# A two-layer hybrid diffusion trunk on one core: a fourth load buffer, and the last half-step's front one token tile at a time

## The chip, the core and the metric

The kernel runs on one core of a Trainium2 chip. Its engines are TensorE (PE, with PEld for loading the stationary operand), VectorE (DVE), ScalarE (ACT), GpSimd (POOL) and SyncE (SP), which here issues nearly all DMAs. The metric is the device time of one execution in microseconds (us), the median of several runs. TensorE's clock has two levels, 1.2 and 2.4 GHz; the profile gives the granted clock of a stretch as a share of the higher.

## The reference

The inputs are 256 latent tokens `x`, 256 context tokens `ctx`, a conditioning vector `c`, and the weights of two layers; width 1024, hidden width 2816, everything in float32. Each layer is a SwiGLU half-step, token mixing, and another SwiGLU half-step. Every sub-layer reads a normalised, shifted and scaled input and is added back through a gate:

```python
def sandwich_in(x, mods, idx, g_pre):
    shift, scale = mods[3 * idx], mods[3 * idx + 1]
    return rms_norm(x, g_pre) * (1 + scale) + shift
def sandwich_out(x, y, mods, idx, g_post, res_w):
    gate = mods[3 * idx + 2]
    return x + res_w * gate * rms_norm(y, g_post)
def swiglu(h, w1, w2):
    a, b = jnp.split(h @ w1, 2, axis=-1)
    return (jax.nn.silu(a) * b) @ w2
```

The nine modulation vectors of a layer come from `c` through one more matrix (adaLN, 1024 x 9216). Token mixing projects to 16 slices of 128 channels, runs four heads of neighbourhood attention, four pooling groups and four heads of differential attention, each differential head with its own normalisation behind it, and projects the 1024 joined channels back with `w_out`. After the last layer only the 256 latent tokens are returned, so its last half-step has 256 tokens, in two tiles of 128.

## The kernel before

All products keep float32 accuracy by splitting each operand into a high and a low part of TensorE's float32 format; a product is then three matmuls, high x high, low x high and high x low. Weights arrive as units of 512 kB: SP issues a DMA into a raw buffer (L179, L204), ACT copies the high part into a slot (L186), DVE subtracts to get the low part (L191). There are three raw buffers, `raw0` to `raw2`, used in a ring: the load of unit k may go once unit k-3 has been split. adaLN weights use the same ring but are not split; DVE multiplies them by the conditioning and adds them up (L464, L466; eight operations per unit), and every four units TensorE sums over partitions (`red`), ACT copies the row (L474), and TensorE transposes it (L482, `fin`). Slots lie in three tiles `w` and in the large tile `R`, which at other times holds mixing data.

The order is made when the kernel is built. `schedule` merges a main list of steps with side lists by due times; `run` then writes the instructions, each step's loads and splits a little ahead of the step, the loads as far ahead as the ring lets them. A load that waits for its buffer holds SP's queue; a split that waits for its data holds ACT's.

A half-step has 22 hidden tiles of 128. For a hidden tile, `pair` takes two units of `w1` as the stationary operand (128 x 128 blocks) and lets the tokens move: with the last half-step's 256 tokens 2 x 8 x 3 = 48 matmuls of 128 x 256. `hidden` follows: silu on ACT (L590), the product with the second half on DVE (L591), the high part on ACT (L593) and the low part on DVE (L594). The first four pairs are the *front* and stand ahead of the others, because their units are loaded while the mixing still runs.

Before the last half-step stands the last out-projection, `wout_rows`: eight rows of `w_out` in the order of the heads that become ready, six matmuls of 128 x 512 for each row and token tile. The last head is the differential head 7; its subtraction L1009 ends the wait. Behind a tile's last row `tok_end` squares (L519), multiplies by the gate (L521), takes the root (DVE L506, POOL L507), adds to the stream `X` (L524), squares and roots again (L525) and writes the normalised rows `YB` (L526). Then `pre_pair`, once for each quarter of the channels and for both token tiles together, transposes `YB` (L536), applies shift and scale on ACT (L539), and splits into `HH` (L540) and `HL` (L541). The front's matmuls come next. The step `late` held some of its `w1` splits back to 4 us behind the out-projection in the planner's count.

## Time and profile before

| | us |
|---|---|
| median of 3 runs | 1832.28 (1830.18 to 1832.47) |
| profiled execution, its own time | 1824.12 |
| its span, first to last instruction | 1822.3 |
| TensorE busy in the span | 1750.3 (96%) |
| DVE / ACT / POOL busy | 1170.7 / 714.8 / 72.8 |
| mean granted clock | 0.987 |
| DMA moved | 260.19 MB, 143 GB/s over the span |

The profile is of one execution. Busy times are sums of instructions; a window's busy time compared with its length says how long the engine had nothing to do there. PE's matmuls overlap, so their single lengths do not add up, and the pace is read from how many start in a stretch. A wait of PE is put down to the instruction whose result it waited for last.

### The profile page before, as it was taken

To read this page: it belongs to the slowest core of one execution; us is meant where nothing else is said; L and a number is where in the kernel's file an instruction comes from. 1 tells how busy PE (TensorE), PEld (TensorE's weight loads), DVE (VectorE), ACT (ScalarE), POOL (GpSimd) and SP (SyncE) were. 2 spreads that over 40 slices of the span, in tenths; PEclk is the share of its full clock that TensorE was granted. 3 is DMA by queue.
4 is the path that set the end of the run, shared out by engine and by line. 5 is a ranking of instruction groups with operands and counts; after the bars stand their busy time and mean duration, and the time that the engine had idled before them with its cause. 6 is when DMAs were issued, how large, how long until landed. Compare 5 with 4: busy or idle time off the path is not lost.

```text
span 1822.3 us, 24374 instructions
## 1 busy us (share of the span) xinstructions
PE 1750.3 (96%) x9496; PEld 1452.9 (80%) x9496; DVE 1170.7 (64%) x1889; ACT 714.8 (39%) x1244; POOL 72.8 (4%) x128
## 2 busy tenths in 40 slices
PE   4999999999999999999999999999999999969998
PEld 3788777778977779878878798888887897859997
DVE  4756776667367875757758565666765737865553
ACT  3323222235267763323222442322223526654442
POOL 0000000001000400000000000000000100200000
PEclk8999999999999999999999999999999999979999
DMA  7836555554211152656545334645554431255662
GB/s 230 243 116 192 176 173 157 167 171 125 57 47 47 64 171 71 188 163 182 176 148 176 124 105 127 197 122 183 176 161 156 115 69 58 93 151 187 187 187 76
DMA packets 301187, 260.19 MB, mean 143 GB/s; under 512 B 18064, under 2 KB 246160, under 8 KB 301072
## 3 DMA queue, kind: packets, MB, share of 16 engines
q1 hardware_dynamic: 297216, 257.67, 46.5%
q8 instruction: 74, 1.21, 0.3%
q10 hardware_dynamic: 3856, 0.97, 0.2%
q14 instruction: 41, 0.34, 0.1%
HBM read 257.51 MB, written 1.10 MB: 142 GB/s over the span
## 4 chain that ended last, share of the span: by engine, by line
PE 65%; DMA 14%; DVE 12%; ACT 5%; issue 3%; POOL 1%; SPq 0%; ACTq 0%; DVEq 0%; POOLq 0%
PE bank L90 62%; DMA raw<-in_ffn_w_dram 10%; DVE sx L466 3%; DVE R L191 2%; ACT R L186 2%; DVE w L191 2%; DMA raw<-in_w_ada_dram 2%; ACT w L186 1%; DMA gtb<-in_w_ada_dram 1%; POOL sr L507 1%; PE bank L802 1%; PE bank L536 1%; DMA csrc<-in_c_dram 1%; DVE sx L464 0%; DVE X L524 0%
## 5 line engine op out<-in xcount | busy, mean ns | idle before, releaser
L90 PE MATMUL bank<-HH,R 128*128 128x512 f32 (+1 forms) x2028 | 531.7, 347 | 4.7 <-ACT R L186 2.5
L90 PE MATMUL bank<-HH,w 128*128 128x512 f32 (+1 forms) x1540 | 433.9, 359 | 0.4 <-DVE w L191 0.4
L90 PEld LDWEIGHTS bank<-HH,R 128*128 128x128 f32 x2028 | 356.3, 191 | 59.5 <-issue 7.2
L90 PE MATMUL bank<-R 128*128 128x512 f32 (+3 forms) x1632 | 364.1, 376 | 2.9 <-DVE YB L642 1.1
L90 PE MATMUL bank<-HL,R 128*128 128x512 f32 (+1 forms) x1014 | 349.5, 345 | 0.0
L90 PEld LDWEIGHTS bank<-R 128*128 128x128 f32 (+1 forms) x1632 | 278.5, 188 | 74.0 <-issue 9.7
L191 DVE TENSOR_TENSOR R<-raw,R 128x1024 fp32r<-128x1024 f32 (+1 forms) x177 | 214.7, 1216 | 173.5 <-ACT R L186 170.1
L466 DVE SCALAR_TENSOR_TENSOR sx<-raw,sc,sx 128x512 f32<-128x512 f32 x448 | 310.8, 745 | 21.8 <-DMA raw<-in_w_ada_dram 21.4
L186 ACT CAST R<-raw 128x1024 fp32r<-128x1024 f32 (+1 forms) x177 | 184.3, 1043 | 343.3 <-DMA raw<-in_ffn_w_dram 270.3
L90 PEld LDWEIGHTS bank<-HH,w 128*128 128x128 f32 x1540 | 274.1, 190 | 50.2 <-issue 12.0
L191 DVE TENSOR_TENSOR w<-raw,w 128x1024 fp32r<-128x1024 f32 (+1 forms) x153 | 187.5, 1226 | 161.8 <-ACT w L186 161.5
L90 PE MATMUL bank<-HL,w 128*128 128x512 f32 (+1 forms) x770 | 274.7, 357 | 0.0
L186 ACT CAST w<-raw 128x1024 fp32r<-128x1024 f32 (+1 forms) x153 | 159.9, 1046 | 279.8 <-DMA raw<-in_ffn_w_dram 199.6
L90 PE MATMUL bank<-w,R 128*128 128x512 f32 x960 | 236.0, 396 | 2.6 <-ACT R L1008 1.8
L90 PEld LDWEIGHTS bank<-w,R 128*128 128x128 f32 x960 | 178.1, 189 | 43.4 <-ACT R L1008 2.3
L90 PEld LDWEIGHTS bank<-HL,R 128*128 128x128 f32 x1014 | 193.3, 191 | 22.4 <-DVE HL L541 0.2
L90 PEld LDWEIGHTS bank<-HL,w 128*128 128x128 f32 x770 | 146.5, 190 | 20.6 <-issue 2.3
L591 DVE TENSOR_TENSOR sil<-sil,bank 128x512 f32<-128x512 f32 (+1 forms) x96 | 55.5, 578 | 77.9 <-PE bank L90 77.7
L593 ACT CAST R<-sil 128x512 fp32r<-128x512 f32 (+1 forms) x96 | 51.2, 533 | 135.0 <-DVE sil L591 135.0
L507 POOL TENSOR_TENSOR sr<-sr,eps 128x1 f32<-128x1 f32 x42 | 28.3, 674 | 1463.5 <-DVE sr L506 1444.5
L590 ACT ACTIVATE sil<-bank 128x512 f32<-128x512 f32 (+1 forms) x96 | 48.9, 510 | 90.7 <-PE bank L90 84.4
L360 DVE TENSOR_TENSOR R<-bank,R 128x512 fp32r<-128x512 f32 (+2 forms) x86 | 47.9, 561 | 33.8 <-ACT R L359 33.5
(145 smaller groups left out, 1211.8 us busy)
## 6 DMA issues: line engine op xcount, KB each, us to landing
raw<-in_ffn_w_dram SPq DMA_DIRECT2D x258, 512.0 KB
raw<-in_w_ada_dram SPq DMA_DIRECT2D x130, 512.0 KB
raw<-in_w_in_dram SPq DMA_DIRECT2D x40, 512.0 KB
raw<-in_w_out_dram SPq DMA_DIRECT2D x24, 512.0 KB
gtb<-in_w_ada_dram SPq DMA_DIRECT2D x10, 512.0 KB
gtb<-gate SPq DMA_DIRECT2D x10, 512.0 KB
raw<-in_ffn_w_dram SPq DMA_DIRECT2D x8, 384.0 KB
sx<-in_w_ada_dram SPq DMA_DIRECT2D x4, 512.0 KB
```

The source lines that it names most:

```text
L90: return nc.tensor.matmul(out=o, lhsT=l, rhs=r, start=start, stop=stop)
L186: ins = S.copy(out=self.hi, in_=self.raw)
L191: ins = self.lo_eng.tensor_tensor(out=self.lo, in0=self.raw, in1=self.hi.bitcast(F32), op=ALU.subtract)
L360: V.tensor_tensor(out=lo, in0=src, in1=hi.bitcast(F32), op=ALU.subtract)
L466: V.scalar_tensor_tensor(out=ACC[v], in0=u.raw[:, z, :], scalar=sv, in1=ACC[v], op0=ALU.mult, op1=ALU.add)
L507: G.tensor_tensor(out=a, in0=a, in1=mhalf, op=ALU.pow)
L536: nc.tensor.transpose(out=pt[:, z, t * P : (t + 1) * P], in_=y[:, t, k * P : (k + 1) * P], identity=ident)
L590: S.activation(out=sl[:, cs], in_=oa, func=AF.Silu)
L591: V.tensor_tensor(out=sl[:, cs], in0=sl[:, cs], in1=ob, op=ALU.mult)
L593: tab["hs"] = S.copy(out=uh[:, cs], in_=sl[:, cs])
L802: nc.tensor.transpose(out=b[:, n * P : (n + 1) * P], in_=e[:, n * P : (n + 1) * P], identity=ident)
```

## The change

1. A fourth raw buffer. Room for it comes from the scratch tile `junk`, which is halved, and from the place of one hidden tile in `R`.
2. adaLN: the transposes of a row (`fin`) are written two units later (`take`); the small loads of the gate's bias are written two units later too.
3. Layout of `R`: hidden units 0 to 7 lie in its first 8192 columns, the ninth at its end, and the load slots between, where they cover whole mixing tiles.
4. Last layer's `wout_rows`: its eight units have fixed slots, each free from a named mark in the mixing; rows 4 to 6 of token tile 1 become low-priority side steps, and its row 7 follows tile 0's.
5. Last half-step's front: token tile by token tile. `pre_tok` prepares half the channels of one tile. `front_tok` keeps `HH` and `HL` blocks of 128 tokens stationary and lets `w1` move, 512 columns at a time: 48 matmuls of 128 x 512 for each tile. The result has tokens on partitions, so `turned` applies silu and product, transposes four blocks and splits them from there into the hidden units. The `late` mark is gone.

```diff
-    raws = [tile(f"raw{i}", [1024]) for i in range(3)]
+    raws = [tile(f"raw{i}", [1024]) for i in range(4)]
-    JUNK = tile("junk", [D], mybir.dt.bfloat16)
+    JUNK = tile("junk", [T], mybir.dt.bfloat16)
-    U_HI = [R[:, i * 1024 : i * 1024 + T] for i in range(NU)]
+    U_AT = [i * 1024 for i in range(8)] + [19456]
+    U_HI = [R[:, i : i + T] for i in U_AT]
...
-                if j % 3 == 2:
-                    st.append(Step(lambda l=l, j=j, h=h: gate_rows(l, j, h)))
                 for q in range(4):
+                    if q == 2 and j % 3 == 2:
+                        st.append(Step(lambda l=l, j=j, h=h: gate_rows(l, j, h)))
...
+    def pre_tok(l, i, g, t, q):
+        ks, ts = slice(4 * q, 4 * q + 4), slice(GROUPS[g].start + t * P, GROUPS[g].start + (t + 1) * P)
+        pt, f = [z.rearrange("p (k t) -> p k t", k=4) for z in (XB(), S2())]
+        for z in range(4):
+            nc.tensor.transpose(out=pt[:, z], in_=y_of(g)[:, t, (4 * q + z) * P : (4 * q + z + 1) * P], identity=ident)
+        for z in range(4):
...
+            if z % 2:
+                V.tensor_scalar(out=f[:, z], in0=pt[:, z], scalar1=sc_, scalar2=sh, op0=ALU.mult, op1=ALU.add)
+            else:
+                S.activation(out=f[:, z], in_=pt[:, z], func=AF.Identity, scale=sc_, bias=sh)
+        V.tensor_copy(out=HH[:, ks, ts], in_=f)
+        V.tensor_tensor(out=HL[:, ks, ts], in0=f, in1=HH[:, ks, ts].bitcast(F32), op=ALU.subtract)
...
-        nf = 0 if done else FRONT
+        nf = 0 if done or not both else FRONT
...
+            fu = [[unit(w1[q * SEQ : (q + 1) * SEQ, h * DFF : h * DFF + T]) for h in range(2)] for q in range(4)]
+            for u in fu[0] + fu[1]:
+                u.after = f"nav{l}"
+            def turned(t, ts, oa, ob):
+                sl = SIL()
+                S.activation(out=sl, in_=oa, func=AF.Silu)
+                V.tensor_tensor(out=sl, in0=sl, in1=ob, op=ALU.mult)
+                pt = XB().rearrange("p (j t) -> p j t", j=4)
+                for j in range(4):
+                    nc.tensor.transpose(out=pt[:, j], in_=sl[:, j * P : (j + 1) * P], identity=ident)
+                u4 = R[:, 0:4096].rearrange("p (j x) -> p j x", j=4)
+                split_ps(u4[:, :, ts], u4[:, :, ts.start + T : ts.stop + T], pt)
...
+                            for oh, u in zip(o, fu[q]):
+                                mm(oh, HH[:, k, ts], u.hi[:, z], k == 0, False)
+                                mm(oh, HL[:, k, ts], u.hi[:, z], False, False)
+                                mm(oh, HH[:, k, ts], u.lo[:, z], False, k == KD - 1)
+                        if q == 3:
+                            turned(t, ts, *o)
...
+            if last:
+                n = 4
+                for i, sl in enumerate((0, 1, 2, 6, 4, 7, 5, 3)):
+                    us[i].slots = (sl,)
+                    if sl > 2:
+                        us[i].after = {6: f"nav{l}", 4: "dv0", 7: "qk0", 5: "dv1", 3: "pt"}[sl]
...
+                t0, t1 = [[row(i, t) for i in range(n, KD)] for t in range(2)]
+                for z in t1[:-1]:
+                    z.low = True
+                t1[-1].needs += t1[:-1]
+                return st + t0, t1, box
...
+            for s in f(*pieces.pop(0)):
+                if s.fin:
+                    late = [s, 2]
+                    continue
+                o.append(s)
+                if late:
+                    late[1] -= 1
+                    if not late[1]:
+                        o.append(late[0])
+                        late = []
...
-            late = Step(lambda: None, after=[(out_[LAT], 4.0)])
-            late.mark = "late"
-            schedule(main + wait_h(f[0][LAT], hl), [late] + hl + side)
+            for t, (end, bks) in enumerate(zip(out_["ends"], (lambda: banks[4:6], lambda: out_["box"]["b"][0]))):
+                main += [Step(lambda t=t, q=q: pre_tok(l, 2, LAT, t, q), dur=0.44, after=[(end, KN["wt"] + q)]) for q in range(2)]
```

Where the instructions stand, at three places. First TensorE at the first adaLN row behind the start, before the change (`rows` is the row that ACT copied, `cst` holds the identity, `bank` a PSUM bank):

```order
L90 MATMUL bank_104<-HL,R 128x512
L90 MATMUL bank_104<-HH,R 128x512
L482 MATMUL bank_106<-cst,rows 128x128 x2
L90 MATMUL bank_105<-HH,R 128x512
L90 MATMUL bank_105<-HL,R 128x512
L90 MATMUL bank_105<-HH,R 128x512 x2
```

and after it:

```order
L90 MATMUL bank_101<-HL,w_72 128x512
L90 MATMUL bank_101<-HH,w_72 128x512
L484 MATMUL bank_107<-cst,rows 128x128 x2
L90 MATMUL bank_101<-HH,w_72 128x512
L90 MATMUL bank_101<-HL,w_72 128x512
L90 MATMUL bank_101<-HH,w_72 128x512 x2
```

The transposes stood between two hidden tiles of one load and now stand 26 rows further on, among matmuls of a later unit; the other rows keep their order.

Next TensorE from the last rows of the last out-projection into the front, before:

```order
L90 MATMUL bank_103<-w_71,R 128x512 x2
L90 MATMUL bank_100<-w_71,R 128x512 x2
L90 MATMUL bank_101<-w_71,R 128x512 x2
L90 MATMUL bank_102<-w_71,R 128x512 x2
L536 MATMUL bank_106<-cst,YB 128x128
L536 MATMUL bank_107<-cst,YB 128x128
L536 MATMUL bank_106<-cst,YB 128x128 x3
L536 MATMUL bank_107<-cst,YB 128x128 x3
L536 MATMUL bank_106<-cst,YB 128x128 x4
L90 MATMUL bank_104<-HH,R 128x256
L90 MATMUL bank_104<-HL,R 128x256
L90 MATMUL bank_104<-HH,R 128x256 x2
```

and after, where the front's first tile begins, and where its second does:

```order
L90 MATMUL bank_101<-R 128x512 x2
L90 MATMUL bank_102<-R 128x512 x2
L90 MATMUL bank_103<-R 128x512 x2
L551 MATMUL bank_107<-cst,YB 128x128 x4
L551 MATMUL bank_108<-cst,YB 128x128 x4
L90 MATMUL bank_105<-w_72,HH 128x512
L90 MATMUL bank_105<-w_72,HL 128x512
L90 MATMUL bank_105<-w_72,HH 128x512
L90 MATMUL bank_106<-w_73,HH 128x512
```

```order
L90 MATMUL bank_106<-R,HH 128x512
L90 MATMUL bank_106<-R,HL 128x512
L90 MATMUL bank_106<-R,HH 128x512
L551 MATMUL bank_108<-cst,YB 128x128 x4
L698 MATMUL bank_107<-cst,sil_75 128x128 x4
L551 MATMUL bank_107<-cst,YB 128x128 x4
L90 MATMUL bank_104<-w_72,HH 128x512
L90 MATMUL bank_101<-w_73,HH 128x512
L90 MATMUL bank_104<-w_72,HL 128x512
L90 MATMUL bank_104<-w_72,HH 128x512
```

Before, transposes of both token tiles go ahead of a front whose weights in `R` are stationary. After, eight transposes of tile 0 go ahead of its 48 matmuls; behind them stand tile 1's first four, the four of `turned`, tile 1's other four, and then tile 1's 48.

Last DVE in the same place, from the end of tile 0 of the out-projection, before (L191 is a load's subtraction, L526 writes a tile's `YB`; tile 0 ends at the fifth row):

```order
L191 TENSOR_TENSOR w_71<-raw_69,w_71 128x1024
L524 SCALAR_TENSOR_TENSOR X<-s_77,sr_84,X 128x512 x2
L191 TENSOR_TENSOR w_73<-raw_68,w_73 128x1024
L506 SCALAR_TENSOR_TENSOR sr_84<-sr_84,eps 128x1
L526 TENSOR_SCALAR YB<-X,sr_84 128x1024
L191 TENSOR_TENSOR w_72<-raw_70,w_72 128x1024
L521 TENSOR_TENSOR s_77<-bank_101,gtb 128x512
L521 TENSOR_TENSOR s_77<-bank_102,gtb 128x512
L506 SCALAR_TENSOR_TENSOR sr_85<-sr_85,eps 128x1
L524 SCALAR_TENSOR_TENSOR X<-s_77,sr_85,X 128x512 x2
L506 SCALAR_TENSOR_TENSOR sr_85<-sr_85,eps 128x1
L526 TENSOR_SCALAR YB<-X,sr_85 128x1024
```

and after (L193 is the subtraction, L529 writes `YB`, L556, L559 and L560 are of `pre_tok`):

```order
L193 TENSOR_TENSOR R<-raw_68,R 128x1024
L509 SCALAR_TENSOR_TENSOR sr_85<-sr_85,eps 128x1
L529 TENSOR_SCALAR YB<-X,sr_85 128x1024
L524 TENSOR_TENSOR s_78<-bank_102,gtb 128x512
L524 TENSOR_TENSOR s_78<-bank_103,gtb 128x512
L509 SCALAR_TENSOR_TENSOR sr_86<-sr_86,eps 128x1
L527 SCALAR_TENSOR_TENSOR X<-s_78,sr_86,X 128x512 x2
L556 TENSOR_SCALAR s_78<-bank_107,A_118,mod_112 128x128
L509 SCALAR_TENSOR_TENSOR sr_86<-sr_86,eps 128x1
L529 TENSOR_SCALAR YB<-X,sr_86 128x1024
L556 TENSOR_SCALAR s_78<-bank_107,A_118,mod_112 128x128
```

```order
L559 CAST HH<-s_78 128x4x128
L560 TENSOR_TENSOR HL<-s_78,HH 128x4x128
L556 TENSOR_SCALAR s_78<-bank_108,A_118,mod_112 128x128
L559 CAST HH<-s_78 128x4x128
L560 TENSOR_TENSOR HL<-s_78,HH 128x4x128
L695 TENSOR_TENSOR sil_75<-sil_75,bank_106 128x512
L556 TENSOR_SCALAR s_78<-bank_108,A_118,mod_112 128x128
L362 TENSOR_TENSOR R<-bank_107,R 128x4x128
L556 TENSOR_SCALAR s_78<-bank_108,A_118,mod_112 128x128
L559 CAST HH<-s_78 128x4x128
```

Four subtractions stood between tile 0's last matmul and tile 1's `YB`, three of them in these rows; two stand there now, the second in the first row shown. Tile 0's `HH` is written behind tile 1's `YB`, and the multiplication of `turned`, L695, stands ahead of tile 1's `HH`.

## Rows read from the trace of the kernel before

**Rows 1.** Of the page's first part, busy time, share and instructions of each engine:

```profile
PE 1750.3 (96%) x9496; PEld 1452.9 (80%) x9496; DVE 1170.7 (64%) x1889; ACT 714.8 (39%) x1244; POOL 72.8 (4%) x128
```

**Rows 2.** Windows: length, PE busy, PEld, DVE, ACT, POOL, clock, DMA, GB/s:

```profile
0.00:75.00 75.00, 50.28 (x430) 37.70 (x431) 41.69 (x97) 26.25 (x48) 3.43 (x12) 0.93 0.86 246
20.00:22.00 2.00, 1.93 (x37) 1.36 (x35) 2.00 (x4) 0.00 (x0) 0.00 (x0) 1.00 0.00 0
100.00:450.00 350.00, 340.56 (x1584) 272.03 (x1583) 239.43 (x364) 104.78 (x157) 6.91 (x11) 0.99 0.52 161
640.00:720.00 80.00, 75.09 (x493) 67.46 (x492) 55.94 (x86) 44.02 (x84) 5.44 (x8) 1.00 0.43 132
720.00:925.00 205.00, 201.74 (x948) 163.26 (x947) 131.83 (x192) 57.95 (x76) 0.00 (x0) 0.99 0.55 170
1150.00:1175.00 25.00, 25.00 (x117) 20.08 (x116) 17.49 (x26) 8.35 (x12) 0.00 (x0) 1.00 0.59 183
1601.50:1625.50 24.00, 7.86 (x24) 5.34 (x25) 16.05 (x24) 13.65 (x27) 2.21 (x4) 0.63 0.68 197
1625.50:1651.00 25.50, 25.50 (x201) 25.25 (x200) 14.51 (x21) 11.75 (x20) 0.00 (x0) 0.94 0.40 124
1630.00:1639.00 9.00, 9.00 (x76) 8.93 (x76) 4.96 (x6) 4.02 (x6) 0.00 (x0) 1.00 0.37 114
```

**Rows 3.** Windows, the first and last stretch behind a wait (columns as above):

```profile
236.30:239.20 2.90, 2.83 (x8) 2.35 (x9) 2.90 (x7) 0.51 (x2) 0.00 (x0) 0.50 0.26 61
...
815.70:818.70 3.00, 2.96 (x9) 2.38 (x10) 3.00 (x6) 0.47 (x1) 0.00 (x0) 0.56 0.43 152
```

**Rows 4.** Timeline of PE: start, length, operation, [wait and its releaser]:

```profile
209.96 0.44 PE L482 MATMUL bank<-cst,rows 128*128 128x128 f32 x2 [0.51 <-ACT rows L474]
...
236.37 0.69 PE L482 MATMUL bank<-cst,rows 128*128 128x128 f32 x2 [2.63 <-ACT rows L474]
...
355.20 0.78 PE L90 MATMUL bank<-HH,R 128*128 128x512 f32 x1 [1.96 <-ACT R L186]
...
815.74 0.44 PE L482 MATMUL bank<-cst,rows 128*128 128x128 f32 x2 [2.12 <-ACT rows L474]
```

**Rows 5.** Chain of waits, 300 to 360: start, length, what:

```profile
330.30 4.75 DMA raw<-in_ffn_w_dram
...
349.10 4.93 DMA raw<-in_ffn_w_dram
...
354.11 1.05 ACT R L186
...
355.19 1.24 DVE R L191
```

**Rows 6.** Waits of ACT, 100 to 450: total us, times, longest:

```profile
ACT R L186 <- DMA raw<-in_ffn_w_dram: 89.7, 27, 10.4
```

**Rows 7.** Timeline of ACT, the last out-projection:

```profile
1599.56 1.06 ACT L186 CAST R<-raw 128x1024 fp32r<-128x1024 f32 x1 [0.53 <-DMA raw<-in_ffn_w_dram]
1601.81 1.04 ACT L186 CAST R<-raw 128x1024 fp32r<-128x1024 f32 x1 [1.20 <-DMA raw<-in_ffn_w_dram]
```

**Rows 8.** Timeline of DVE, last out-projection to last half-step:

```profile
1607.54 1.22 DVE L191 TENSOR_TENSOR R<-raw,R 128x1024 fp32r<-128x1024 f32 x1 [0.30 <-ACT R L186]
...
1615.49 1.22 DVE L191 TENSOR_TENSOR w<-raw,w 128x1024 fp32r<-128x1024 f32 x1
...
1621.93 0.75 DVE L526 TENSOR_SCALAR YB<-X,sr 128x1024 f32<-128x1024 f32 x1 [0.66 <-POOL sr L507]
1624.73 0.43 DVE L540 CAST HH<-s 128x512 fp32r<-128x512 f32 x1 [2.05 <-ACT s L539]
```

**Rows 9.** Of the page's fifth part, costliest groups: busy, mean ns, idle before:

```profile
L591 DVE TENSOR_TENSOR sil<-sil,bank 128x512 f32<-128x512 f32 (+1 forms) x96 | 55.5, 578 | 77.9 <-PE bank L90 77.7
...
L590 ACT ACTIVATE sil<-bank 128x512 f32<-128x512 f32 (+1 forms) x96 | 48.9, 510 | 90.7 <-PE bank L90 84.4
L360 DVE TENSOR_TENSOR R<-bank,R 128x512 fp32r<-128x512 f32 (+2 forms) x86 | 47.9, 561 | 33.8 <-ACT R L359 33.5
```

More of the change, by code (lines that the diff above doesn't have):

```diff
@@ L658, in tail_of @@
             return st
-        nf = 0 if done else FRONT
+        nf = 0 if done or not both else FRONT
         fr = [w1_units(j) for j in range(nf)]
-        if l == DEPTH - 1 and f == 1:
-            for u in [u for p in fr for u in p][KN["nh"]:]:
-                u.after = "late"
         for j in range(nf):
@@ L670, in ffn, with front_tok, fn @@
         if not both:
+            fu = [[unit(w1[q * SEQ : (q + 1) * SEQ, h * DFF : h * DFF + T]) for h in range(2)] for q in range(4)]
[10 more added lines that the diff above has]
+                split_ps(u4[:, :, ts], u4[:, :, ts.start + T : ts.stop + T], pt)
+            def front_tok(t, bks):
+                ts = slice((2 + t) * P, (3 + t) * P)
+                st = []
+                for q in range(4):
+                    def fn(q=q):
+                        o = bks()
+                        for z in range(2):
+                            k = 2 * q + z
+                            for oh, u in zip(o, fu[q]):
[4 more added lines that the diff above has]
+                            turned(t, ts, *o)
+                    st.append(Step(fn, fu[q], 12 * T / 2400.0))
+                return st
+            front = front_tok
             yb = [banks[0:2], banks[2:4]]
@@ L1063, in rows, with row, fn @@
                     mm(o, MIXH[:, k, ts], wl, False, i == KD - 1)
+            if last:
[4 more added lines that the diff above has]
+                        us[i].after = {6: f"nav{l}", 4: "dv0", 7: "qk0", 5: "dv1", 3: "pt"}[sl]
+                def row(i, t):
+                    def fn():
+                        rows(i, t)
+                        if i == KD - 1:
+                            tok_end(g, t, box["b"][t], False)
+                    return Step(fn, [us[i]], 6 * T / 2400.0, after=[mixed[ks[i], g]])
+                for i in range(n):
+                    st += [Step(lambda: None, us[i + 1 : i + 2]), row(i, 0), row(i, 1)]
+                t0, t1 = [[row(i, t) for i in range(n, KD)] for t in range(2)]
[3 more added lines that the diff above has]
+                return st + t0, t1, box
             def ending(t, n):
@@ L1148, in mixing @@
             rows = wout_rows(g, order)
-            end = rows[-1]
             mk = Step(lambda: None, needs=[z for it in items for z in it] + prods + subs)
             mk.mark = f"ffn{l}1"
+            if last:
+                rows, t1, box = rows
+                for name, z in ((f"nav{l}", prods[:4]), ("dv0", prods[:6]), ("qk0", [it[0] for it in boxes[4]["items"]]),
+                                ("dv1", prods), ("pt", prods + [it[1] for it in items])):
+                    side.append(Step(lambda: None, needs=list(z)))
+                    side[-1].mark = name
+                main += rows[:-1] + [mk, rows[-1]]
+                side += t1[:-1]
+                main.append(t1[-1])
+                out_ = {"ends": (rows[-1], t1[-1]), "box": box}
+                break
+            end = rows[-1]
             if g == out_groups[-1]:
@@ L1185, in x_stat @@
         for t in range(2):
-            S.activation(out=JUNK, in_=xs[g][:, t], func=AF.Square, scale=RMS, accum_out=st[:, t : t + 1])
+            S.activation(out=S2T, in_=xs[g][:, t], func=AF.Square, scale=RMS, accum_out=st[:, t : t + 1])
         if g == LAT:
@@ L1287, in take @@
     def take(n, f=ada_v):
-        o = []
+        o, late = [], []
         for _ in range(n):
-            o += f(*pieces.pop(0))
-        return o
+            for s in f(*pieces.pop(0)):
[8 more added lines that the diff above has]
+                        late = []
+        return o + late[:1]
     body = f[1]
@@ L1308, in hybrid_trunk @@
         if last:
-            hl = chain(l, 2, LAT, out_[LAT], KN["wt"])
-            late = Step(lambda: None, after=[(out_[LAT], 4.0)])
-            late.mark = "late"
-            schedule(main + wait_h(f[0][LAT], hl), [late] + hl + side)
+            for t, (end, bks) in enumerate(zip(out_["ends"], (lambda: banks[4:6], lambda: out_["box"]["b"][0]))):
+                main += [Step(lambda t=t, q=q: pre_tok(l, 2, LAT, t, q), dur=0.44, after=[(end, KN["wt"] + q)]) for q in range(2)]
+                fr = f[0](t, bks)
+                fr[0].after.append((main[-2], 2.0))
+                fr[2].after.append((main[-1], 2.0))
+                main += fr
+            schedule(main, side)
             body = f[1]
```

16 lines of the change are left out of this document (9 added, 7 removed).

## The prediction

> **What bounds the kernel now.** I read the page first: TensorE is busy 96% of the span [rows 1]. So this change can gain in two ways only, by filling TensorE's 72 idle us or by giving it less or faster work. The windows by stage then say where those 72 us lie [rows 2]: 24.7 in the first 75 us, where the DMA share is 0.86; 9.4 in 100–450 and 3.3 in 720–925, where weights stream past at 161 and 170 GB/s; 4.9 in 640–720, from the first layer's out-projection to the half-step behind it; 16.1 in 1601.5–1625.5, between the last out-projection and the last half-step. The stages between them hardly wait.
>
> Next the clock column. After a wait TensorE has its lower level, 1.2 of 2.4 GHz: four such stretches lie in the two streaming stages, the first at 236.3–239.2 with a mean clock of 0.50, the last at 815.7–818.7 with 0.56 [rows 3]. These two lose 2.9 x 0.50 + 3.0 x 0.44 = 2.8 us, the two between them as much or a little more, 5.8 in all. So a stall of 2 us costs 3.4.
>
> Who ends the waits? PE's timeline has two kinds [rows 4]: a transpose of the adaLN row (L482) that waits for the row copy on ACT, and a weight matmul that waits for ACT's cast (L186). The chain of waits behind the second kind shows the ring of three load buffers at its limit [rows 5]: 4.75 to 4.93 us of DMA, 1.05 of cast, 1.24 of subtraction, and at that end the next load into the same buffer is issued. One turn is 4.75 + 1.05 + 1.24 + some 0.3 of waits = 7.3 us, 2.4 per load with three buffers. The stream needs one load of 524 kB every 3.3 us at 161 GB/s. That leaves a quarter of slack, which an adaLN load uses up when its vector operations come in a lump behind others. The first kind of wait has the same root: ACT takes its work in order and stood at casts whose data had not landed, 89.7 us of the 350 [rows 6], and the row copy stood behind one of them.
>
> **Part by part.** *A fourth buffer, and the adaLN transpose two loads later.* The order of all TensorE work in 100–450 and 720–925 stays, except that L482's pair stands some 27 rows later, about 8 us at 0.214 a matmul. One turn with four buffers is 1.8 us per load against 3.3 needed. At stake are 9.4 + 3.3 idle and 5.8 of slow clock, 18.5 us. The lower bound is 6 (only the three L482 waits of [rows 4], 0.51 + 2.63 + 2.12 = 5.3, and a little of their slow clock), the upper 18.5. I take two thirds, 12.3: the chain in [rows 5] is of buffers throughout, but ACT stands at casts wherever the planner writes them, and a few waits (L593 for the multiplication, L642) have no buffer in them.
>
> *Start.* DMA lies still for 2.0 us at 20–22 [rows 2], while SyncE waits for a buffer. The fourth takes that load at once. But the next one waits for the old buffers again: 1.0 of the 2.0 us, bounds 0 and 1.4.
>
> *First layer, out-projection to half-step (640–720).* Idle 4.9. The order is unchanged, and two of its four waits are token-wise chains without any load; one follows an ACT wait on a load. I take 2.0, bounds 0 and 4.
>
> *Second tile's rows held back.* In the order all held matmuls (rows 4 to 6 of tile 1) stand ahead of tile 0's last row, where they fill the wait for the last head. Behind tile 0 come six matmuls, as before. So this covers nothing of the 16.1 us, and I cost it at nothing: the total of matmuls is the same. The w_out weights go into slots of R that come free early, so they load sooner; this takes the place of loads that were there anyway.
>
> *Last out-projection.* ACT waited 0.53 and 1.20 at casts ahead of the last head's output [rows 7]. With a buffer more these loads have landed: 1.7 earlier.
>
> *Way to the front.* Before, the chain from tile 0's last matmul to tile 1's normalised rows has four subtractions of 1.22 between its own steps (the first and the last stand in [rows 8], as does YB at 1621.93), and the front begins with the stretch 1625.5–1651 of [rows 2], 2.8 behind YB's end at 1622.68. Now two subtractions are left there: -2.4. Tile 0's affine and cast stand behind tile 1's normalisation on DVE, so the front still waits for both; but it needs one tile's half instead of both: two short affine steps (an estimate of 0.35 each, below the 0.43 of the four times longer cast L540 in [rows 8]), a 0.43 cast and some 0.3 between them, 1.4 instead of 2.8: -1.4. Together -3.8.
>
> *Pace.* Before, 4 pairs x 2 x 8 x 3 = 192 matmuls of 256 columns, 76 in the 9 us of 1630–1639 [rows 2], 0.12 each: 23.0. Now 96 of 512 columns, 117 in 25 us [rows 2], 0.214 each: 20.5. -2.5.
>
> *A new wait between the tiles.* Tile 1's front stands behind `turned` of tile 0: silu 0.51, multiplication 0.58, subtraction 0.56 [rows 9], the cast of the same size on ACT as long as the silu, then four transposes, and the affine and the cast of tile 1, which DVE takes only after these, some 0.43 each like L540 in [rows 8]: 3.5, with seven hand-overs of 0.1, 4.2. No work of TensorE stands in between. If DVE had finished tile 1's halves before, only silu and multiplication would be left, 1.3 (bound). After it the clock may fall as in [rows 3]: the front before paid that too, once (25.5 us at 0.94 in [rows 2]); now twice perhaps, half a chance of 1.4, 0.7. The second tile's four transposes 0.5; those of tile 0 lie in the wait.
>
> Last stage: -1.7 - 3.8 - 2.5 + 4.2 + 0.7 + 0.5 = -2.6, bounds -6.2 and +3.0 (no earlier loads, no subtraction gone from the chain, the wait 5.0, the full slow clock).
>
> **Sum.** 12.3 + 1.0 + 2.0 + 2.6 = 17.9 us off the profiled execution's 1824.1: 1806.2. The median of the three runs is 1832.28, 1.0045 times that execution, so 1814.3, say **1814**.
>
> **Rivals.** (1) *The fourth buffer brings nothing.* Casts are written into ACT's order by the planner and ACT stands at each till its data is there; if the transfer and not the turn of the buffer is late, one more buffer changes no cast, and the wait that L482 loses falls on the next matmul that needs the late cast. For it: [rows 6]. Against: [rows 5], where each load is issued at the end of a subtraction. Left are the short L482 wait of 0.5 and the last stage: 1824.1 - 3.1 = 1821.0, 1829.2 by the median. A rule of the Trainium skill gives that: its page "DMA: Bandwidth & Descriptors", section "Anatomy of one DMA — SWDGE (gpsimd) path", puts one transfer at 2.0 us and its bytes at 436 GB/s, by which I estimate 3.2 us for 524 kB. A turn would then be 5.5 us, 1.8 per load with three buffers already, and the stalls would not come from the ring. The trace disagrees: the loads in [rows 5] take 4.75 to 4.93 us, several under way at once. I give it 0.12.
>
> (2) *The front by tiles loses* (last stage at its bound, +3.0): 1824.1 - 15.3 + 3.0 = 1811.8, by the median 1819.9. For it: the DVE order puts `turned` ahead of tile 1's cast. Against: 3.8 us of the chain go in any case. 0.16.
>
> (3) *Slower.* One more buffer lets the planner write casts earlier into ACT's order, in part ahead of silu and eviction copies. Where four loads are in flight each takes longer (DMA share is 0.52 on average but 0.86 at the start), and an earlier cast whose data is late holds the silu, and TensorE behind it. Each such place costs 2.0 and 1.4 of slow clock, as in [rows 4]. It decides once there are more than five new ones, which eat the 17.9 us; with as many new ones as there are now and the old left, 1824.1 + 18.5 - 2.6 = 1840.0, by the median 1848. Against: the planner takes out-of-need casts only when it believes them landed. 0.07.
>
> **Chances.** Forecast 0.62, rivals 0.12, 0.16 and 0.07; 0.03 for a mixture near nothing or a larger gain than 18.5. A measurement of this kernel tells a difference of some 0.2% from none, 3.7 us: faster is below 1828.6, slower above 1835.9. Forecast and rival 2 are faster, 0.78, with a share of the rest 0.80; rival 1, just above 1828.6, mostly the same, 0.13; slower 0.07. Range: the terms at their good ends together give 18.5 + 1.4 + 4 + 6.2 = 30.1, which would be 1802 by the median; at their bad ends they end near rival 1. With that rival and the second inside: **1804 to 1830**.
>
> **What would show it.** In the trace after: the ring, by ACT's waits at casts in 100–450 well under 90 us and no stretch of 3 us at half clock like those of [rows 3]; the start, by no two us without DMA; the last stage, by the front's first matmul some 5.5 us sooner behind tile 0's last head, a wait of about 4 us between two blocks of 48 matmuls, and 20.5 us for both. I am wrong if the stalls of 2 us stand at the same places, then rival 1; or if new ones of ACT stand at silu or eviction behind a cast, then rival 3.

## The result and the profile after

The changed kernel takes 1814.13 us (median of 4 runs, 1812.20 to 1819.16) where the kernel before takes 1832.12: a ratio of 0.9908, 95% interval 0.9887 to 0.9929, so 13 to 21 us less. The forecast was 1814. The time is right. The working behind it is right in its largest term, and wrong in the smaller ones and in the step from the profile to the median; these two errors happened to cancel.

The first thing to see is that the two profiles do not show those 18 us. The profiled execution after took 1814.39 us (span 1812.6), which is close to its median. That of before took 1824.12, and timed runs of that kernel, on this and later chips, lie between 1823.96 and 1835.47. So the trace of before was of a short execution, and the traces differ by 9.7 us only.

The windows of the kernel after, to be held against [rows 2] (length, busy PE, PEld, DVE, ACT, POOL, clock, DMA share, GB/s; the last two stretches are from tile 0's last matmul to the front, and the front):

```profile
20.00:22.00 2.00, 2.00 (x29) 1.59 (x31) 2.00 (x4) 0.00 (x0) 0.00 (x0) 1.00 0.26 95
100.00:450.00 350.00, 345.09 (x1668) 279.43 (x1667) 245.29 (x375) 110.76 (x167) 7.46 (x11) 1.00 0.55 164
640.00:720.00 80.00, 75.23 (x516) 68.53 (x515) 50.65 (x78) 40.12 (x77) 4.86 (x8) 0.98 0.43 124
720.00:925.00 205.00, 204.11 (x935) 164.38 (x934) 141.18 (x209) 55.65 (x75) 0.00 (x0) 1.00 0.57 171
1594.10:1609.10 15.00, 3.33 (x15) 2.35 (x13) 11.54 (x22) 8.94 (x22) 2.22 (x4) 0.66 0.60 191
1609.10:1638.60 29.50, 27.57 (x109) 21.50 (x110) 13.11 (x19) 8.05 (x12) 0.00 (x0) 0.88 0.18 56
```

In 100–450 TensorE's idle time fell from 9.4 to 4.9 us, in 720–925 from 3.3 to 0.9, and the clock of both reads 1.00. In 640–720 nothing moved: 4.8 idle instead of 4.9. Of the 4.9 us left in 100–450, 2.03 are one wait for normalised rows, which has no load in it:

```profile
438.90 0.87 PE L539 MATMUL bank<-cst,YB 128*128 128x128 f32 x6 [2.03 <-DVE YB L529]
```

ACT's waits for the data of a cast stand in two rows, of which [rows 6] shows one, the casts into `R`, with 89.7 us. The casts into `w` before, and both rows after (total, times, longest):

```profile
ACT w L186 <- DMA raw<-in_ffn_w_dram: 78.8, 19, 11.3
...
ACT R L188 <- DMA raw<-in_ffn_w_dram: 50.3, 21, 7.1
ACT w L188 <- DMA raw<-in_ffn_w_dram: 39.6, 16, 9.0
```

Together they fell from 168.5 to 89.9 us.

The front is another matter. PE's timeline around it (start, length, operation, idle time before it and its releaser):

```profile
1601.91 1.97 PE L551 MATMUL bank<-cst,YB 128*128 128x128 f32 x8 [6.48 <-DVE YB L529]
1609.07 0.79 PE L90 MATMUL bank<-w,HH 128*128 128x512 f32 x1 [5.19 <-DVE HH L559]
...
1618.29 0.62 PE L90 MATMUL bank<-R,HH 128*128 128x512 f32 x2
...
1618.97 0.62 PE L90 MATMUL bank<-R,HH 128*128 128x512 f32 x2
...
1622.92 0.66 PE L698 MATMUL bank<-cst,sil 128*128 128x128 f32 x4 [0.41 <-DVE sil L695]
1624.98 0.66 PE L551 MATMUL bank<-cst,YB 128*128 128x128 f32 x4 [1.40 <-DVE R L362]
1625.76 0.76 PE L90 MATMUL bank<-w,HH 128*128 128x512 f32 x2
...
1641.68 0.55 PE L698 MATMUL bank<-cst,sil 128*128 128x128 f32 x3 [1.76 <-DVE sil L695]
```

Three waits stand there: 0.41 and 1.40 between the two tiles, around transposes that finish one tile and prepare the next, and 1.76 behind the second tile, at the transposes of `turned` (L698), which wait for DVE's multiplication L695. From tile 0's last matmul, whose first square on ACT starts at 1594.16 (1605.83 before), to the end of the span the kernel after takes 1812.6 - 1594.2 = 218.4 us; the kernel before took 216.5. In this pair of profiles that last stage lost 1.9 us where the forecast had it gain 0.9 (its 2.6 without the 1.7 ahead of that matmul); a second pair, e9 and e1 below, makes it 0.3.

### The profile page after: what moved, and what is told of

Read it like the earlier page. It is cut to its first block, busy times and chain, and to the rows that moved or that the text cites. A ratio compares the mean times of both kernels' runs of the same rounds, so it can differ in the third digit from the quotient of the medians.

```text
span 1812.6 us, 24180 instructions
## 1 busy us (share of the span) xinstructions
PE 1747.6 (96%) x9408; PEld 1447.9 (80%) x9408; DVE 1171.1 (65%) x1893; ACT 713.1 (39%) x1240; POOL 76.3 (4%) x128
## 4 chain that ended last, share of the span: by engine, by line
PE 77%; DMA 8%; DVE 7%; ACT 4%; issue 2%; POOL 2%; ACTq 0%; DVEq 0%; POOLq 0%
PE bank L90 74%; DMA raw<-in_ffn_w_dram 6%; ACT R L188 1%; DVE R L193 1%; DVE w L193 1%; DMA gtb<-in_w_ada_dram 1%; ACT w L188 1%; POOL sr L510 1%; PE bank L852 1%; PE bank L539 1%; DVE sx L468 1%; DVE X L527 1%; DMA csrc<-in_c_dram 1%; DMA raw<-in_w_in_dram 1%; DVE YB L529 0%
## 5 line engine op out<-in xcount | busy, mean ns | idle before, releaser
L90 PE MATMUL bank<-HH,R 128*128 128x512 f32 (+1 forms) x1932 | 511.0, 349 | 1.2 <-ACT sil L609 1.2
L90 PE MATMUL bank<-HH,w 128*128 128x512 f32 (+1 forms) x1508 | 427.1, 360 | 0.0
L90 PEld LDWEIGHTS bank<-HH,R 128*128 128x128 f32 x1932 | 340.2, 190 | 53.9 <-issue 7.2
L90 PE MATMUL bank<-R 128*128 128x512 f32 (+3 forms) x1680 | 375.2, 377 | 4.6 <-ACT YB L659 1.6
L90 PEld LDWEIGHTS bank<-R 128*128 128x128 f32 (+1 forms) x1680 | 286.7, 188 | 79.1 <-issue 9.5
L90 PE MATMUL bank<-HL,R 128*128 128x512 f32 (+1 forms) x966 | 335.0, 347 | 0.0
L193 DVE TENSOR_TENSOR R<-raw,R 128x1024 fp32r<-128x1024 f32 (+1 forms) x180 | 218.2, 1216 | 177.7 <-ACT R L188 175.3
L90 PEld LDWEIGHTS bank<-HH,w 128*128 128x128 f32 x1508 | 268.1, 189 | 49.2 <-issue 11.6
L193 DVE TENSOR_TENSOR w<-raw,w 128x1024 fp32r<-128x1024 f32 (+1 forms) x150 | 183.5, 1227 | 140.0 <-ACT w L188 139.7
L188 ACT CAST w<-raw 128x1024 fp32r<-128x1024 f32 (+1 forms) x150 | 156.4, 1046 | 228.8 <-DMA raw<-in_ffn_w_dram 131.0
L90 PE MATMUL bank<-w,R 128*128 128x512 f32 x912 | 223.4, 396 | 1.4 <-DVE YB L661 0.8
L90 PEld LDWEIGHTS bank<-w,R 128*128 128x128 f32 x912 | 169.5, 189 | 39.7 <-DVE YB L661 1.2
L90 PEld LDWEIGHTS bank<-HL,R 128*128 128x128 f32 x966 | 183.3, 190 | 21.9
```

Of the source, the lines that this page charges most:

```text
L90: return nc.tensor.matmul(out=o, lhsT=l, rhs=r, start=start, stop=stop)
L188: ins = S.copy(out=self.hi, in_=self.raw)
L193: ins = self.lo_eng.tensor_tensor(out=self.lo, in0=self.raw, in1=self.hi.bitcast(F32), op=ALU.subtract)
```

## The experiments

All were timed in five rounds against the kernel before on the same chip. "Last stage" is, in the run's profile, the time from the first square behind tile 0's last matmul to the end of the span. Two profiles of the same kernel differ in it by up to 1.1 us. In e1 that square stood behind a cast whose data came 2.07 us late, so its 217.5 is rather too short.

| run | what it is | median us | ratio, 95% interval | last stage us |
|---|---|---|---|---|
| e1 | before, again | 1828.58 | 0.9990 (0.9976–1.0005) | 217.5 |
| e2 | before, four buffers | 1815.73 | 0.9925 (0.9908–0.9942) | 215.4 |
| e3 | before, late transposes | 1825.42 | 0.9972 (0.9962–0.9982) | 217.2 |
| e4 | before, both of these | 1811.96 | 0.9898 (0.9881–0.9915) | 215.9 |
| e5 | after, three buffers | 1828.58 | 0.9990 (0.9976–1.0004) | 221.2 |
| e6 / e10 | after, front by pairs | 1809.06 / 1809.37 | 0.9883 (0.9865–0.9901) / 0.9888 (0.9869–0.9906) | 214.4 / 214.1 |
| e9 | after, again | 1814.42 | 0.9917 (0.9902–0.9932) | 217.8 |
| e7 | after, `turned` late | 1809.06 | 0.9883 (0.9865–0.9901) | 211.5 |
| e8 / e11 | the same, tile 0 first | 1806.06 / 1806.64 | 0.9872 (0.9851–0.9892) / 0.9874 (0.9855–0.9893) | 211.5 / 210.8 |
| e12 | the same, waits filled | 1802.81 | 0.9860 (0.9838–0.9881) | 209.6 |

### The kernel before once more (e1)

No edit.

> The kernel before, unchanged, once more with a profile. Its first profiled execution took 1824.1 us, the timed runs 1830.2 to 1832.5, while the changed kernel's profiled execution lies at its median. Theory A (executions of this kernel differ by 8 us, and the first profile was of a short one): the new profile has its own time of 1830 to 1832, with the extra 6 to 8 us in named stages, as more waits behind the load ring or more stretches at half clock. Theory B (a profiled execution of this kernel is always shorter than a timed one): again 1824, the same stalls at the same places. Ratio 0.998 to 1.002 under both.

Its profiled execution took 1826.97 us, its other runs 1825.43 to 1835.29. PE's timeline at two of the places of [rows 4], and the windows of the two streaming stages:

```profile
235.98 0.44 PE L482 MATMUL bank<-cst,rows 128*128 128x128 f32 x2 [2.87 <-ACT rows L474]
...
816.35 0.44 PE L482 MATMUL bank<-cst,rows 128*128 128x128 f32 x2 [2.32 <-ACT rows L474]
```

```profile
100.00:450.00 350.00, 338.42 (x1573) 269.13 (x1571) 238.11 (x363) 104.70 (x157) 6.90 (x11) 0.99 0.54 160
720.00:925.00 205.00, 200.91 (x953) 162.83 (x952) 131.76 (x193) 58.83 (x78) 0.00 (x0) 1.00 0.57 170
```

The stalls behind the row copy stand at the same places and are longer: 2.87 for 2.63 at 236, 2.32 for 2.12 at 816. Idle are 11.6 us for 9.4 in 100–450 and 4.1 for 3.3 in 720–925. That is theory A for the 2.9 us by which this span is longer than the first, though the 1830 to 1832 that it named did not come. A profile of one of the executions near 1832 was not taken, so that their further 5 us lie at the same waits is argued and not shown.

### Four buffers alone (e2)

```diff
-    raws = [tile(f"raw{i}", [1024]) for i in range(3)]
+    raws = [tile(f"raw{i}", [1024]) for i in range(4)]
...
-    JUNK = tile("junk", [D], mybir.dt.bfloat16)
+    JUNK = tile("junk", [T], mybir.dt.bfloat16)
...
```

The squares at the start write to another scratch tile, since `junk` is shorter. `R` is laid out as before: the fourth buffer fits without the place of a hidden tile in `R` that item 1 of the change names.

> The kernel before with four load buffers and nothing else. Theory (the ring of three sets the waits in the streaming stages): 9 to 13 us less, ratio 0.993 to 0.995, TensorE at 1046 us some 9 to 12 earlier, the waits for the adaLN row copy shorter but not all gone. Rival (the late transposes take the waits away, the buffer nothing): 0 to 3 us less, ratio above 0.998.

13.7 us less (0.0075 of 1830.84), a little more than the upper expectation. The rival is out. The windows, the one wait for the adaLN row copy above 0.5 us that is left behind the start, with the longest wait of that stage, and what ACT does just ahead of the first:

```profile
100.00:450.00 350.00, 346.28 (x1692) 281.81 (x1691) 247.25 (x378) 113.09 (x169) 7.45 (x11) 1.00 0.55 164
720.00:925.00 205.00, 199.29 (x898) 159.60 (x897) 130.42 (x194) 52.43 (x69) 0.00 (x0) 0.98 0.53 162
```

```profile
830.12 0.44 PE L482 MATMUL bank<-cst,rows 128*128 128x128 f32 x2 [2.21 <-ACT rows L474]
...
904.70 10.53 PE L90 MATMUL bank<-R 128*128 128x512 f32 x38 [3.00 <-DVE YB L642]
```

```profile
828.73 1.05 ACT L186 CAST R<-raw 128x1024 fp32r<-128x1024 f32 x1 [1.88 <-DMA raw<-in_ffn_w_dram]
829.69 0.38 ACT L474 ACTIVATE rows<-bank 128x256 f32<-128x256 f32 x1
```

In 100–450 the idle time is 3.7 us. In 720–925 it is 5.7, more than before: at 830 a cast waited 1.88 for its data and the row copy L474 stood behind it. So four buffers do not end this kind of wait altogether. The longer wait, 3.00 at 904.70, is for DVE's addition L642, which was 1.14 in the first profile of before and 1.77 in e1; why it grew is not shown. A fifth buffer was not tried.

### The late transposes alone (e3)

```diff
...
+                if s.fin:
+                    late = [s, 2]
+                    continue
...
```

This is item 2 of the change as a whole: the small loads of the gate's bias are two units later too, and what they do by themselves was not measured.

> The kernel before with the adaLN transposes two loads later and nothing else, three buffers. Theory: the three waits behind the row copy go (5.3 us) with 2.8 of half clock, but the waits for casts stay or take over: 2 to 6 us less, ratio 0.997 to 0.999. Rival (the late transposes are what counts): 10 us or more less, ratio at or below 0.9945.

5.1 us less, within the theory's 2 to 6. No wait behind the row copy above 0.5 us is left behind the start, but new ones for casts are there. The largest two of the new ones:

```profile
316.01 0.50 PE L90 MATMUL bank<-HH,w 128*128 128x512 f32 x1 [2.76 <-ACT w L186]
```

```profile
1254.89 0.50 PE L90 MATMUL bank<-HH,R 128*128 128x512 f32 x1 [1.66 <-ACT R L186]
```

```profile
1100.00:1300.00 200.00, 196.49 (x910) 157.61 (x909) 120.97 (x179) 54.79 (x72) 0.00 (x0) 0.99 0.51 153
```

The second, and the 0.53 behind it, stand where the kernel before did not wait: its 1100–1300 was busy for all 200 us, here for 196.5. That takes back some of the gain.

### Both (e4)

The edits of e2 and e3 together, nothing else.

> Both of the last two and nothing else; the last half-step as before. Theory: what the changed kernel gains up to the last out-projection, 12 us in the two first profiles, and nothing lost behind it: 1814 to 1819 us by the median, ratio 0.991 to 0.9935. Rival (part of the gain needs the new layout and the pinned out-projection units): ratio above 0.995.

18.7 us less, more than the theory's 12 to 16.5, and just what the two give one by one (13.7 + 5.1). No part of these 18.7 us needs the new layout or the pinned units. This alone is no slower than the whole change, 0.9898 against 0.9908 and, again, 0.9917; the intervals overlap.

```profile
100.00:450.00 350.00, 343.70 (x1665) 278.79 (x1664) 245.26 (x375) 110.63 (x167) 7.45 (x11) 1.00 0.55 163
720.00:925.00 205.00, 204.01 (x935) 164.34 (x934) 140.77 (x209) 55.39 (x73) 0.00 (x0) 1.00 0.57 171
```

In 720–925 the idle time is down to 1.0, where e2 had 5.7: neither of e2's two waits is left. In 100–450 it is 6.3, more than e2's 3.7 and less than the 9.4 of before.

### The change with three buffers (e5)

```diff
-    raws = [tile(f"raw{i}", [1024]) for i in range(4)]
+    raws = [tile(f"raw{i}", [1024]) for i in range(3)]
```

> The changed kernel with three load buffers instead of four, all else as changed. Theory (buffer and late transposes add up, 15 and 5 us, and the last half-step's parts give nothing or cost 1 to 2): the transposes' 5 us less and the rest nothing, ratio 0.997 to 0.999. Rival (pinned units and early w_out loads also bring something with three buffers): ratio 0.994 to 0.996.

0.9990: within the theory, at its upper end. Against e3 it is 3.3 us slower by the ratios, and its last stage is the longest of all, 221.2. With three buffers the rest of the change is more likely a loss than a gain; the intervals of e3 and e5 overlap.

### The front by pairs (e6, e10) beside the changed kernel (e9)

```diff
-        nf = 0 if done or not both else FRONT
+        nf = 0 if done else FRONT
-            front = front_tok
...
+            hl = chain(l, 2, LAT, out_["ends"][1], KN["wt"])
+            schedule(main + wait_h(f[0][LAT], hl), hl + side)
```

> The changed kernel with its four buffers, late transposes, layout and pinned out-projection units, but with the last front by pairs for both token tiles, as before. Theory (the front by tiles costs: from tile 0's last head to the end it took 218.4 us in the changed kernel's profile, 216.5 in that of the kernel before): ratio 0.987 to 0.990, the stretch from the last head to the end 212 to 215 because two subtractions are gone from the way to the front. Rival (the front by tiles gains in the median of runs): ratio 0.991 or more.

> The changed kernel with the front by pairs again, beside the changed kernel on one chip. Theory: ratio 0.987 to 0.9895, 3 to 6 us below the run before it. Rival: within 2 us of it.

> The changed kernel again, on the chip of the next three. Theory (the front by tiles as it is ordered costs 4 us, its other parts gain 2 to 3 over buffer and late transposes alone): ratio 0.990 to 0.992, 3 to 6 us above the next run. Rival (the front by tiles costs nothing, and the difference between 0.9908 and 0.9883 was that of two chips): within 2 us of the next run.

On one chip the changed kernel took 1814.42 us and the same kernel with the front by pairs 1809.37: the front by tiles costs 5.0 us as it is ordered. The two sets of executions lie apart, 1813.21 to 1816.30 and 1807.43 to 1811.43. The last stages say 217.8 and 214.1. The other parts of the change (layout, pinned units, held rows) bring 1.8 to 2.7 us over e4 by the ratios, inside the intervals of both, so that gain is likely and not settled.

### `turned` later, tile 1 prepared earlier (e7)

`turned` is cut in two. Silu and multiplication stay; transposes and split become a step of their own behind the next block's first 12 matmuls (for tile 1 behind the first 24 of pair 4). Tile 1's `pre_tok` goes ahead of the second half of tile 0's front.

```diff
-                main += fr
...
+            main += pre[0] + frs[0][:2] + pre[1] + frs[0][2:] + frs[1][:1] + f[0].turn[:1] + frs[1][1:]
...
+            body.insert(4, f[0].turn[1])
```

> The changed kernel with the front by tiles, but tile 1's preparation written before the second half of tile 0's front, and the transposes of turned written after the first 12 matmuls of the next block (after 24 of the next pair for tile 1). Theory (the wait of 3.9 us between the tiles, the half clock behind it, 2.5 us, and the wait of 1.8 us behind tile 1 come from the order alone): 6 to 8 us less than the changed kernel, ratio 0.9865 to 0.9885, no wait above 0.3 us between the two blocks of 48. Rival (something else, as weights that are not there, holds TensorE between the tiles): ratio as the changed kernel's, 0.990 to 0.992.

The ratio is 0.9883, within the theory; that is 4.6 to 6.2 us less than the changed kernel in its two measurements, mostly under the 6 to 8 expected. It is also the ratio of the front by pairs on the same chip (e6), so by the medians the better order only catches up with it. The last stage is 2.9 us shorter than e6's. PE's timeline where tile 0's block (weights in `R`) ends and tile 1's (weights in `w`) begins:

```profile
1623.63 0.39 PE L90 MATMUL bank<-R,HH 128*128 128x512 f32 x1
1623.86 0.39 PE L90 MATMUL bank<-w,HH 128*128 128x512 f32 x1
...
1626.58 0.60 PE L703 MATMUL bank<-cst,sil 128*128 128x128 f32 x4
```

Tile 1's block follows without a wait at full clock, the transposes (L703) stand 12 matmuls on, and no wait is left behind tile 1 either. The waits of the changed kernel between and behind the tiles came from the order of its instructions, not from missing weights.

### Tile 0's cast ahead of tile 1's normalisation (e8, e11)

```diff
+                t1.append(Step(lambda: tok_end(g, 1, box["b"][1], False, SX[:, :D])))
```

Tile 1's `tok_end` uses another scratch tile than tile 0's affine, and is written behind tile 0's first `pre_tok`.

> As the last one, and tile 1's end of the out-projection has a scratch tile of its own, so that tile 0's cast no longer stands behind tile 1's normalisation on DVE. Theory: the front begins 3 to 4 us earlier behind tile 0's last matmul, ratio 0.984 to 0.987. Rival (the front then reaches tile 1 before its rows are there): the 3 to 4 us come back as a wait in front of tile 1's block, ratio as the last one's.

> The front by tiles in its better order (tile 1 prepared early, transposes of turned late, tile 0's cast ahead of tile 1's normalisation) again. Theory: ratio 0.986 to 0.988, the fastest of this call but for the next run; its stretch from the last head to the end 211 to 212 us. Rival (no better than the front by pairs): the two intervals lie on each other, within 1 us.

0.9872 and 0.9874, against 0.9883 for e7: the intervals overlap, and the last stage is 211.5 and 210.8 against 211.5. So the gain that e8's theory wanted, to 0.987 at most, is not shown. The front did begin earlier, 12.9 and 12.6 us behind tile 0's last matmul instead of 15.4. The rival I had named (tile 1's rows not there) did not come either. Half of the time went to the clock, as the windows from the front's start show (e11), with the transposes of tile 1 behind them:

```profile
1605.10:1610.60 5.50, 5.50 (x13) 4.30 (x14) 2.87 (x6) 0.01 (x1) 0.93 (x1) 0.50 0.00 1
1610.60:1613.00 2.40, 2.40 (x11) 1.97 (x11) 0.00 (x0) 0.00 (x0) 0.00 (x0) 1.00 0.00 0
```

```profile
1613.25 1.03 PE L552 MATMUL bank<-cst,YB 128*128 128x128 f32 x8
```

And the same of e7:

```profile
1611.10:1613.80 2.70, 2.70 (x8) 2.15 (x7) 2.63 (x7) 0.96 (x3) 0.00 (x0) 0.50 0.00 0
1613.80:1616.00 2.20, 2.20 (x11) 1.79 (x10) 1.10 (x2) 0.00 (x0) 0.00 (x0) 0.99 0.00 0
```

Here the front's first 5.5 us run at 0.50, in e7 its first 2.7, so 2.8 us are lost instead of 1.4. The low stretch ended 18.1 us behind tile 0's last matmul here and 18.0 in e7. And all eight transposes of tile 1 stand among the front's matmuls, where e7 has four of them in the wait ahead of the front: some 0.4 us more. Against the front by pairs on the same chip e11 is 2.7 us faster and e8 3.0, with overlapping intervals.

### The waits filled (e12)

```diff
+            def warm(n):
+                def fn():
+                    for _ in range(n):
+                        mm(banks[4].rearrange("p (a t) -> p a t", a=2), HH[:, 0, 0:P], HH[:, 0:2, 0:SEQ], True, True)
+                return Step(fn)
```

34 matmuls whose result nothing reads: the planner puts one among tile 1's last row, 26 behind it, 7 behind tile 0's transposes.

> The last one with 34 more matmuls of 128 x 512 whose result is not used, 27 of them behind tile 1's last row and 7 behind tile 0's transposes, where TensorE waits for DVE. They take 7 us of its idle time. Theory (the front began at the lower clock because TensorE had stood still, 6 us of it at half clock in the last one, so 3 us lost): no or a shorter stretch at 0.50 in the front, 1.5 to 3 us less, ratio 0.984 to 0.987. Rival (the clock has another reason, as what DVE and ACT do there): the same half clock and the same time, or 1 to 2 us more because the matmuls delay the transposes.

1802.81 us, 0.9860. The last stage is 1.2 us shorter than in e11, the median 3.8. The intervals overlap, and 1.2 is hardly more than two profiles of one kernel differ by, so the time gained is likely and not settled; what is plain is the clock. PE's timeline and windows, the first of e11, the others of this run:

```profile
1592.19 6.05 PE L90 MATMUL bank<-HH 128*128 128x512 f32 x26
1598.84 1.09 PE L552 MATMUL bank<-cst,YB 128*128 128x128 f32 x8 [0.60 <-DVE YB L530]
1599.69 1.86 PE L90 MATMUL bank<-HH 128*128 128x512 f32 x7
1603.35 0.73 PE L90 MATMUL bank<-w,HH 128*128 128x512 f32 x2 [1.80 <-DVE HH L560]
```

```profile
1600.00:1605.00 5.00, 1.97 (x8) 1.57 (x8) 4.30 (x11) 2.90 (x9) 0.55 (x1) 0.50 0.51 193
...
1600.00:1605.00 5.00, 3.02 (x12) 1.89 (x11) 4.31 (x11) 2.78 (x7) 1.13 (x2) 1.00 0.33 109
1605.00:1610.00 5.00, 5.00 (x16) 3.94 (x16) 1.35 (x2) 0.00 (x0) 0.09 (x1) 0.66 0.00 0
```

TensorE stays at 1.00 through the chain, where it was at 0.50 in e11's 1600–1605, and the front's first matmuls run at full pace. Then the low level comes all the same, in 1605–1610, behind the 1.80 us wait that was left, and is shorter: 5 x 0.34 = 1.7 us lost instead of 2.8. The theory (standing still costs the clock) agrees with this. The gain is smaller than it said; that the wait which was left is the reason is argued and not shown.

## Why the prediction was right, and where it was not

**Buffer and late transposes, 12.3.** Right in mechanism: the ring of three sets the stalls of the streaming stages (e2), and the late transposes take what a fourth buffer leaves (e2 at 830, e4). By the profiles the kernel is 12.4 us earlier from 1046 us on (tile rows of the second layer's first half-step: 1046.07 before, 1033.71 after), close to the 12.3 with the start in it. By the medians the two are worth 18.7 (e4). Rival 1 is out. The fit of the Trainium skill in "DMA: Bandwidth & Descriptors", section "Anatomy of one DMA — SWDGE (gpsimd) path", is per DMA, measured on GpSimd's path. SP issues these loads, several under way at once, and for them the prediction's estimate of 3.2 us from that fit, by which a fourth buffer would have been worthless, does not hold: they take 4.75 to 4.93 us [rows 5], and the buffer is worth 13.7 us here. The Trainium skill, "Perfetto Trace Analysis", section "Optimization Strategy", says that a gap which repeats on the engine that should be saturated can mean too few buffers; e2 agrees, with the same 13.7 us.

**Start 1.0 and 640–720 2.0.** The DMA share in 20–22 rose from 0.00 to 0.26 only. TensorE's idle time up to 90 us was 24.7 and 23.8 in the two profiles of before and 23.8 in that of after: no gain can be told. In 640–720 there was none (4.8 for 4.9): the wait behind an ACT wait on a load fell only from 1.29 to 0.79, at 674, and the two token-wise ones are 1.62 and 1.06, where they were 1.67 and 1.24. 3.0 us of the sum were not there. The five stretches of the prediction's first paragraph hold 58.4 of the 72 idle us; the other 13.6 lie in stages that it says hardly wait, and no term is for them.

**The last stage, -2.6.** The gain did not come. Against the kernel before, the last stage is 218.4 us for 216.5 in the first pair of profiles and 217.8 (e9) for 217.5 (e1) in the second, 0.3 to 1.9 more where 0.9 less was forecast. Against the front by pairs, all else equal, the front by tiles costs 5.0 us (e9, e10). Term by term, by the first pair:

| term | forecast | measured in the trace after |
|---|---|---|
| loads ahead of the last head | -1.7 | none: TensorE's last wait for the head's cast is 1.33 for 1.85, but tile 0's last matmul lies 11.7 earlier, less than the 12.4 of the stages ahead |
| way to the front | -3.8 | -4.8 (14.9 us for 19.7) |
| pace | -2.5 | -1.2 |
| wait between the tiles | +4.2 | +3.85 (1621.91 to 1625.76) |
| clock | +0.7 | +2.0 |
| `turned` of tile 1 | +0.5 | +2.2 |

Of the pace: I took 117 matmuls in 25 us from a stretch of the first half-steps' kind. In the front three matmuls take 0.68 us (1618.29 to 1618.97), 0.227 each, so 96 take 21.8 and not 20.5. Of the clock: in this execution both blocks began with a low stretch, not one and a half. The stretches, the first also up to its end:

```profile
1609.07:1612.70 3.63, 3.63 (x8) 2.61 (x9) 2.11 (x4) 0.10 (x1) 0.00 (x0) 0.50 0.00 0
1609.07:1614.50 5.43, 5.43 (x16) 4.08 (x17) 2.11 (x4) 0.10 (x1) 0.00 (x0) 0.67 0.00 0
1625.70:1631.00 5.30, 5.24 (x15) 3.91 (x16) 3.02 (x7) 2.44 (x4) 0.00 (x0) 0.68 0.00 0
```

They lose 5.4 x 0.33 + 5.3 x 0.32 = 3.5 us; the front before lost 25.5 x 0.06 = 1.5. In the second execution of the same kernel (e9), behind the same waits of 0.41 and 1.40 between the tiles, it was the first block alone, and for longer:

```profile
1608.79:1614.40 5.61, 5.61 (x13) 4.11 (x14) 2.11 (x4) 0.10 (x1) 0.00 (x0) 0.50 0.00 0
1626.51:1631.00 4.49, 4.49 (x19) 3.41 (x19) 3.51 (x6) 2.84 (x4) 0.00 (x0) 1.00 0.00 0
```

That is 2.8 us, and +1.3 for the term. Of `turned`: I had costed its transposes behind tile 1 at their own length, because pair 4 follows, and had not looked at what stands ahead of the silu on ACT and ahead of the multiplication on DVE. Those two engines, in the kernel after:

```profile
1638.73 1.05 ACT L188 CAST R<-raw 128x1024 fp32r<-128x1024 f32 x1 [1.63 <-DMA raw<-in_ffn_w_dram]
1639.68 0.59 ACT L694 ACTIVATE sil<-bank 128x512 f32<-128x512 f32 x1
```

```profile
1639.81 1.23 DVE L193 TENSOR_TENSOR R<-raw,R 128x1024 fp32r<-128x1024 f32 x1 [1.46 <-ACT R L188]
1640.95 0.68 DVE L695 TENSOR_TENSOR sil<-sil,bank 128x512 f32<-128x512 f32 x1
```

The silu stood behind a cast whose data came 1.63 us late, and the multiplication behind that cast's subtraction. SP had issued nothing since 1603.4, and then ten loads in a row:

```profile
1631.79 17.74 SPq L181 DMA_DIRECT2D raw<-in_ffn_w_dram  x10
```

The front by tiles reads all eight `w1` units for tile 0 and again for tile 1, so no slot comes free until its second block, and then the loads come in a lump. By pairs a unit is done after 24 matmuls of 0.12. That is a cost of the front by tiles that no term of mine had. It is not why e5 with three buffers has the longest last stage: the same wait is 1.45 there, and its front begins 17.6 us behind tile 0's last matmul instead of 14.9.

**The held rows, 0.** The order had shown that they cover nothing behind tile 0, and the 6.48 us wait ahead of L551 is still there. Shown by the trace.

**From the profile to the median, x 1.0045.** The sum, 17.9, was of waits in one short execution, of which 9.7 came. The other 8 us came from the step that I had taken for a mere change of scale: the changed kernel's profile lies at its median, that of before 8 us below its own. By the medians its usual execution had more to gain than the one that I read. That the buffer takes these waits away too is likely (e2 gains 8.8 us by the first profile of before, 11.6 by the second, 13.7 by the medians). So 1814 was met by luck: two errors of some 8 us cancelled. With one of them alone the forecast would have been 1814.4 x 1.0045 = 1822.6, or 1806.2.

**Rivals 2 and 3.** Rival 2, the front by tiles loses, was the true one in its sign, though the last stage lost 0.3 to 1.9 us and not its 3.0. Its time of 1819.9 did not come because buffer and late transposes brought more by the median (18.7 in e4). Rival 3 is out: in 100–925 TensorE's longest wait for ACT is 0.89 us, where stalls of 2 and more have gone.

## What to carry to other kernels

Where loads, casts and subtractions run through a small ring, read one full turn of a buffer from the chain of waits and divide by the buffers. Here that was a quarter below the time between loads, 2.4 for 3.3 us, and lumps elsewhere still stalled it; one more buffer was worth 13.7 us, the later transposes 5.1. Before computing the same product with larger blocks, look at what the old order did beside its matmuls: it released weights early and spread its silu work. Moving the new transposes behind other matmuls won back the second (e7); the first was not tried. A profile is one execution: compare its own time with the spread of the timed runs before summing up its waits.

## What the runs showed of the hardware

Behind the same kind of wait the low clock came and went differently from one execution to the next. In e7 and e11 it ended 18 us behind tile 0's last matmul, whether the front began at 15.4 or at 12.6. In the changed kernel, whose front began at 14.9 and 15.2, it ended at 18.5 in one execution and at 20.8 in the other (e9). Behind the waits of 0.41 and 1.40 between the tiles it came in the first of these two and not in the second. What fixes its end is not shown. In e11 the 2.8 us of earlier start were worth 0.7 at most.

Matmuls with no use kept the granted clock at 1.00 through a chain of DVE and ACT work (e12, 1600–1605), where it was 0.50 without them (e11).
